# Making weight sums inside the up tiles: GpSimd's load queue, new row shapes, transposes, and a new order of products

## The chip, the cores and the metric

The kernel runs on one core of a Trainium2 chip. The core has five engines that work side by side: TensorE (PE in the profile; its weight loads are shown as PEld), VectorE (DVE), ScalarE (ACT), GpSimd (POOL) and SyncE (SP), and sixteen DMA engines that move data between the chip's memory (HBM) and the core's memory (SBUF). TensorE writes to PSUM, a small memory of eight banks. Each engine executes its own instructions in order; a DMA is issued by an engine's queue and lands later.

The metric is the time of one execution in microseconds of device time, and the median over runs.

## The reference, cut to what matters

A trunk of two layers on 256 tokens of width 2048, in float32. Each layer has a token mixer (first an mLSTM, then an HGRN2) and a gated MLP with a short convolution:

```python
def conv_glu(hn, w_up, conv_w, conv_b, w_down):
    u = hn @ w_up                       # (256, 2048) @ (2048, 11008)
    a, v = jnp.split(u, 2, axis=-1)
    ...
    c = conv_b
    for j in range(CONV_W):             # three taps
        c = c + ap[:, j:j + s] * conv_w[j]
    return (jax.nn.gelu(c, approximate=False) * v) @ w_down    # (256, 5504) @ (5504, 2048)

for layer in range(DEPTH):
    h = h + mix
    h = h + conv_glu(rmsnorm(h, norm_ffn_g[layer]), ffn_w_up[layer], ...)
```

The change touches only the gated MLP and its two matrix products.

## The kernel before, in words

**Precision by halves.** Every weight and activation is split into a rounded part and a remainder (`wh`, `wl`; `xh`, `xl`). A product is three matmuls, wh with xh, wl with xh, and wh with xl. For the weights the split is done on the chip (`halves`, L163): ScalarE copies a piece of 1024 columns to `wh` (L166), VectorE subtracts it from the raw weights to get `wl` (L167). There are four buffers of each (`WB`), and three raw buffers of 2048 columns (`RAW`), which SyncE's queue fills (L157 and L269). TensorE reads the pieces in order, so it can go on for as long as the pieces made ahead last.

**Stages of the MLP.** The 5504 hidden columns are 43 tiles of 128, in three parts of 16, 16 and 11 (`PARTS`). In each part an *up stage* comes first. One up tile is a chunk of kind "fm": 16 steps k over the width 2048, in each step two groups of columns (gate and value), and in each group one matmul of 512 columns (L436) and one of 256 (L439), 64 in all. Then `done_up` (L1100) scales, convolves, applies GELU, multiplies, and splits the result `g`. The second k step of the first up tile of each part is in a "turned" order, both products of 512 columns first and then both of 256 (`TURNS`, L424 to L433); other tiles of the mixers use this order too.

After the up stage come two *pairs* (`Pair`, `stream_pair`, L293), each of which makes 1024 of the 2048 output columns of the part's down product. A pair goes through its hidden tiles in couples. The letters of the plan tell how a couple is computed:

- N: two by two blocks of products, eight in all (H: the half of it).
- S: seven products instead of eight (a Strassen form). They need sums of the four blocks of weights, which `pair_sums` (L229) makes on VectorE in a buffer T4 just before they are used. The products go to four accumulators in two big PSUM tiles (c11, c12, c21, c22) and three small banks of their own (m1, m6, m7). At the last S or P `middle` adds the small ones to the residual stream `hx`, and at the pair's end `done` adds the big tiles (L1180).
- P: the same as S, but the sums were made ahead. The generator `sums_ahead` (L242) takes half a couple at a time: it loads it to the tile `pr0` with SyncE's queue (L253), makes the four sums in `pr1` (L230 to L232), splits them into `pr2` and `pr3` (L256, L257), and stores these two in HBM, in the array `sums`, with GpSimd's queue (L259). A row of such a load or store is 256 columns, 1 KB. When the pair arrives at the couple, GpSimd's queue loads the finished sums back into the same four tiles (L279), and the two plain blocks come through the raw buffers.

Each full pair has the plan PSNSPSNN with two P, each short one PSNNNH with one, and layer 1's last part has only one pair. That makes 19 couples, 38 halves.

**What sets the order.** `side.push` hands a generator to a little clock that advances by the estimated time of each product (`side.tick`); `sums_ahead` begins `REST` = 8 us after the part's first up tile by this clock and takes a half each `EACH` = 12 us. That is the order in which instructions are written. A planner then arranges each engine's instructions by their dependencies and its own estimate of times, and can take an instruction ahead of its place in the program where nothing that it depends on holds it back. On an engine's queue, what is behind a waiting instruction waits too.

Of the kernel before, what the change touches and what calls it, by code (L numbers as in the profile page):

```python
# [15 lines left out]
P = 128  # L16
# [5 lines left out]
TURNS = 1  # L22
# [6 lines left out]
REST = 8.0  # L29
EACH = 12.0  # L30
# [36 lines left out]
def trunk_kernel(ctx, tc, xT, x_d, fg_d, pp_d, cst_d, sel_d, w_gate, w_first, w_aq, w_ak, w_av, w_ao, w_aout,  # L67
# [64 lines left out]
    class Chunk:  # L132
        def __init__(self, kind, src, nk, x, done, before=None, last=False, turns=0):
            self.last, self.turns, self.apart = last, turns, False
            self.kind, self.src, self.nk, self.x, self.done, self.before = kind, src, nk, x, done, before
            self.width = {"fm": 256, "tm": 512, "first": 512}[kind]
# [26 lines left out]
    def halves(r, m):  # L163
        wh = wpool.tile([P, 1024], F32R, tag="wh", bufs=WB, name="wh")
        wl = wpool.tile([P, 1024], F32R, tag="wl", bufs=WB, name="wl")
        act.copy(wh[:, :m], r)  # L166
        dve.tensor_tensor(wl[:, :m], r, wh[:, :m].bitcast(F32), ALU.subtract)  # L167
# [74 lines left out]
    def sums_ahead(srcs, box):  # L242

        yield REST
        due, h = side.now, 256
        for n, src in srcs:
            for o in (0, h):
                while side.now < due and not side.flush:
                    yield 0.1
                due += EACH  # L250
                b, t, th, tl = (spare(i, box) for i in range(4))
                b, t = (v.bitcast(F32).rearrange("p (a b) -> p a b", a=4) for v in (b, t))
                nc.sync.dma_start(b, src.rearrange("p (a b) -> p a b", a=4)[:, :, o:o + h])  # L253
                pair_sums(b, t)
                t = t.rearrange("p a b -> p (a b)")
                act.copy(th, t)  # L256
                dve.tensor_tensor(tl, t, th.bitcast(F32), ALU.subtract)  # L257
                for j, v in enumerate((th, tl)):
                    pool.dma_start(sums[n, j].rearrange("p (a b) -> p a b", a=4)[:, :, o:o + h],  # L259
                                   v.rearrange("p (a b) -> p a b", a=4))  # L260
            stored.append(n)

    def split_pair(ch):
        w, b0 = ch.w, 0
        for kind in ch.plan:
            n = (2 if kind == "H" else 4) * w
            raw = wpool.tile([P, 2048], F32, tag="raw", bufs=RAW, name="raw")
            skip = w if kind == "P" else 0
            nc.sync.dma_start(raw[:, skip:n], ch.src[:, b0 + skip:b0 + n])  # L269
            c, b0 = b0 // n, b0 + n  # L270
            if kind == "P":
                yield halves(raw[:, w:3 * w], 2 * w)
                yield halves(raw[:, 3 * w:4 * w], w)
                n = ch.made[c]
                side.until(lambda: n in stored)
# [5 lines left out]
                continue  # L281
            if kind != "S":
# [10 lines left out]
    def stream_pair(ch, take):  # L293
# [5 lines left out]
        def product(name, x, wt, sp=False):  # L299
            (xh, xl), (wh, wl) = x, wt  # L300
            for i, (a, b) in enumerate(((xh, wh), (xh, wl), (xl, wh))):
                pe.matmul(acc[name][:, 0:w], a, b, start=name not in begun, stop=sp and i == 2)  # L302
# [6 lines left out]
        def part(u, i):  # L309
# [3 lines left out]
        for c, kind in enumerate(ch.plan):  # L313
            end = c == len(ch.plan) - 1
            if kind in "SP":
                kind = "S"
# [7 lines left out]
                u = take()  # L324
                product("m1", tok(k, 0), part(u, 0), fin)
                side.tick(0.68)
                product("c12", form(3), part(u, 1))
                side.tick(0.68)
                u = take()
                product("c11", tok(k + 1, 0), part(u, 0))  # L330
                side.tick(0.68)
                u = take()
                product("c22", form(0), part(u, 0), fin)
                if fin:
                    begun.discard("c22")
                side.tick(0.68)
                product("m7", form(2), part(u, 1), fin)
                side.tick(0.68)
                u = take()
                product("m6", form(1), part(u, 0), fin)  # L340
                side.tick(0.68)
                product("c21", tok(k + 1, 1), part(u, 1))
                if fin:
                    with tc.high_priority():
                        ch.middle(acc)
# [979 lines left out]
```

## Time and profile before

| | us |
|---|---|
| median of 3 runs | 2431.31 |
| lowest, highest run | 2430.45, 2440.63 |
| profiled execution, its own time | 2437.75 |
| its span, first to last instruction | 2435.7 |

| engine | instructions of the largest groups |
|---|---|
| TensorE | products of the "fm" tiles, L436 and L439, 3678 each |
| VectorE | remainders of weights, L167, 829 |
| ScalarE | rounded weights, L166, 829 |
| GpSimd | stores of sums, L259, 76, and loads of sums, L279, 76 |

The mean granted TensorE clock is 0.994 of full speed. The queue of SyncE moved 457.26 MB, GpSimd's 85.01 MB.

How to read the lines: a group or timeline line gives engine, line of the kernel, operation, what is written and read, and in brackets how long the engine was idle before it and what ended that. A line of stretches gives a stretch of time, and for each engine the busy time and number of instructions in it; then the granted clock, the mean busy share of the DMA engines and the GB/s moved. A product's busy time includes waiting in TensorE's pipe, so the number of matmuls in a stretch says more than their busy time.

### The profile page before, as it was taken

What the parts mean: (1) busy time and instruction counts of PE and PEld (TensorE: products, weight loads), DVE (VectorE), ACT (ScalarE), POOL (GpSimd) and SP (SyncE); (2) the same over time, 40 slices, a digit from 0 to 9 for tenths busy, and PEclk for the clock granted to TensorE, in tenths of its full rate; (3) what the DMA queues carried; (4) which work ended last, traced back from release to release, by engine and by line L of the source; (5) the groups of instructions that cost most, each with busy time, mean ns of one, the idle gap of its engine ahead of it and who ended that gap; (6) DMA issues with size and microseconds to landing.
All of it is one profiled execution on the core that took longest, in us unless ns stands there. A gap on an engine that the chain in (4) does not pass through costs nothing.

```text
span 2435.7 us, 37196 instructions
## 1 busy us (share of the span) xinstructions
PE 2398.5 (98%) x14200; PEld 2044.1 (84%) x14200; DVE 1937.7 (80%) x3159; ACT 1335.2 (55%) x2057; POOL 256.6 (11%) x375
## 2 busy tenths in 40 slices
PE   9999999999999999999999999998999999999998
PEld 7888878888888888878888888887888878888887
DVE  7766667778878788778888888886777878879776
ACT  6655556555456555555555555555555545554554
POOL 0100011000010011001222222211000101000000
PEclk9999999999999999999999999999999999999999
DMA  7654489556898589655444554449855789668744
GB/s 292 199 182 173 173 258 329 190 191 217 285 302 284 182 291 297 228 195 192 169 171 171 174 173 162 171 180 284 293 188 179 262 283 299 242 212 286 262 169 172
DMA packets 137633, 545.82 MB, mean 224 GB/s; under 512 B 10720, under 2 KB 69728, under 8 KB 86896
## 3 DMA queue, kind: packets, MB, share of 16 engines
q1 hardware_dynamic: 84288, 457.26, 53.2%
q0 software_dynamic: 52304, 85.01, 12.5%
q8 instruction: 111, 1.82, 0.3%
q10 hardware_dynamic: 864, 1.19, 0.1%
q14 instruction: 66, 0.54, 0.1%
HBM read 501.41 MB, written 42.01 MB: 223 GB/s over the span
## 4 chain that ended last, share of the span: by engine, by line
PE 80%; DMA 7%; DVE 6%; issue 4%; ACT 1%; POOL 0%; SPq 0%; POOLq 0%; ACTq 0%; DVEq 0%
PE mm L436 32%; PE mm L439 16%; PE mm L420 6%; PE mm L419 6%; PE mm L421 6%; PE c L302 6%; DVE wl L167 3%; DMA sums<-pr 3%; PE m L302 2%; DMA raw<-in_w_down 2%; DMA raw<-in_w_up 1%; ACT wh L166 1%; PE mm L428 1%; PE pn L785 1%; PE pd L968 1%
## 5 line engine op out<-in xcount | busy, mean ns | idle before, releaser
L436 PE MATMUL mm<-xt,wh 128*128 128x512 f32 x3678 | 1291.4, 396 | 1.8 <-ACT wh L166 1.8
L167 DVE TENSOR_TENSOR wl<-raw,wh 128x1024 fp32r<-128x1024 f32 (+1 forms) x829 | 990.9, 1200 | 321.3 <-ACT wh L166 314.0
L166 ACT CAST wh<-raw 128x1024 fp32r<-128x1024 f32 (+1 forms) x829 | 842.4, 1025 | 724.8 <-PE mm L436 422.2
L439 PE MATMUL mm<-xt,wl 128*128 128x256 f32 x3678 | 1026.4, 280 | 8.7 <-DVE wl L167 8.7
L436 PEld LDWEIGHTS mm<-xt,wh 128*128 128x128 f32 x3678 | 690.6, 188 | 162.2 <-ACT wh L166 3.4
L439 PEld LDWEIGHTS mm<-xt,wl 128*128 128x128 f32 x3678 | 694.2, 189 | 12.5 <-DVE wl L167 10.1
L302 PE MATMUL c<-wh,g 128*128 128x512 f32 x666 | 218.0, 390 | 0.0
L419 PE MATMUL mm<-wh,xt 128*128 128x512 f32 x480 | 188.1, 392 | 0.0
L420 PE MATMUL mm<-wl,xt 128*128 128x512 f32 x480 | 187.7, 391 | 0.0
L421 PE MATMUL mm<-wh,xt 128*128 128x512 f32 x480 | 187.3, 390 | 0.0
L302 PEld LDWEIGHTS c<-wh,g 128*128 128x128 f32 x666 | 125.3, 188 | 26.1
L302 PE MATMUL c<-wl,g 128*128 128x512 f32 x333 | 130.0, 390 | 0.0
L279 POOL DMA_DIRECT2D pr<-sums x76 | 40.9, 547 | 828.1 <-PE c L302 761.6
L421 PEld LDWEIGHTS mm<-wh,xt 128*128 128x128 f32 x480 | 90.2, 188 | 18.5
L419 PEld LDWEIGHTS mm<-wh,xt 128*128 128x128 f32 x480 | 90.1, 188 | 18.4
L420 PEld LDWEIGHTS mm<-wl,xt 128*128 128x128 f32 x480 | 90.1, 188 | 17.3
L257 DVE TENSOR_TENSOR pr<-pr,pr 128x1024 fp32r<-128x1024 f32 x38 | 46.4, 1222 | 72.1 <-DMA sums<-pr 59.8
L259 POOL DMA_DIRECT2D sums<-pr x76 | 54.2, 713 | 464.3 <-ACT pr L256 390.4
L166 ACT CAST wh<-T 128x1024 fp32r<-128x1024 f32 x54 | 56.1, 1051 | 71.4 <-PE c L302 37.9
L471 ACT COPY b<-mm 128x256 f32<-128x256 f32 x236 | 86.4, 366 | 14.3 <-DVE z L472 6.7
L167 DVE TENSOR_TENSOR wl<-T,wh 128x1024 fp32r<-128x1024 f32 x54 | 65.4, 1223 | 24.7 <-ACT wh L166 24.4
L256 ACT CAST pr<-pr 128x1024 fp32r<-128x1024 f32 x38 | 39.9, 1051 | 77.7 <-DMA sums<-pr 54.3
(269 smaller groups left out, 3001.2 us busy)
## 6 DMA issues: line engine op xcount, KB each, us to landing
raw<-in_w_up SPq DMA_DIRECT2D x172, 1024.0 KB, 5.0
raw<-in_w_down SPq DMA_DIRECT2D x60, 1024.0 KB, 4.9
raw<-in_w_bq SPq DMA_DIRECT2D x48, 1024.0 KB, 4.9
sums<-pr POOLq DMA_DIRECT2D x76, 512.0 KB, 8.3
pr<-sums POOLq DMA_DIRECT2D x76, 512.0 KB, 7.9
pr<-in_w_down SPq DMA_DIRECT2D x38, 512.0 KB, 5.3
raw<-in_w_ao SPq DMA_DIRECT2D x16, 1024.0 KB, 4.7
raw<-in_w_aout SPq DMA_DIRECT2D x16, 1024.0 KB, 6.4
```

The lines of the kernel that those rows point to most:

```text
L166: act.copy(wh[:, :m], r)
L167: dve.tensor_tensor(wl[:, :m], r, wh[:, :m].bitcast(F32), ALU.subtract)
L257: dve.tensor_tensor(tl, t, th.bitcast(F32), ALU.subtract)
L259: pool.dma_start(sums[n, j].rearrange("p (a b) -> p a b", a=4)[:, :, o:o + h], v.rearrange("p (a b) -> p a b", a=4))
L279: pool.dma_start(z[j], sums[n, j][:, 1024 * i:1024 * i + 1024])
L302: pe.matmul(acc[name][:, 0:w], a, b, start=name not in begun, stop=sp and i == 2)
L419: pe.matmul(ps[t], xh, wh[:, c], start=st, stop=False)
L420: pe.matmul(ps[t], xh, wl[:, c], start=False, stop=False)
L421: pe.matmul(ps[t], xl, wh[:, c], start=False, stop=sp)
L436: pe.matmul(ps[f], wh[:, c:c + P], x, start=st, stop=False)
L439: pe.matmul(ps[f][:, 0:T], wl[:, c:c + P], x[:, 0:T], start=False, stop=sp)
L471: act.copy(b, ps[:, T:2 * T])
```

## The change

Five things are different. The whole core of the diff follows.

1. `sums_ahead` is no generator on the clock any more. `done_up` calls it in chosen up tiles (`MAKE`: tiles 1, 2, 4, 5, 7, 8, 10, 11 of a part of 16; 1 to 4 of the part of 11), each time for one half couple. GpSimd first copies one column of that tile's output `c` into the load's buffer, and then issues the load, which therefore can't go before the tile's output is there. The load is on GpSimd's queue, no longer on SyncE's.
2. The weights of P couples are stored in HBM in another order (`_couples`), so that a half couple's row is 4 KB in one piece. The stores of the sums have rows of 2 KB. A P couple's two plain blocks and the first product's block now lie as two halves of 256 columns, so products of P couples read their 512 columns as two runs of 256.
3. In the first couple of each pair the products that go to the small banks come first: m1, m7, m6, c12, c11, c22, c21, where it was m1, c12, c11, c22, m7, m6, c21.
4. The turned order at the start of a part's first up tile is gone. In each up stage two transposes of a constant 128 x 128 matrix into a PSUM bank are put in that nobody reads (`RESETS`: before step k = 1 of tiles 2 and 9 in the first part, before k = 3 of tile 0 and k = 1 of tile 6 in the others).
5. The pool of the four `pr` tiles is opened with the MLP's other tiles.

```diff
-TURNS = 1
+RESETS = (((2, 1), (9, 1)), ((0, 3), (6, 1)), ((0, 3), (6, 1)))
...
-REST = 8.0
-EACH = 12.0
+MAKE = {16: (1, 2, 4, 5, 7, 8, 10, 11), 11: (1, 2, 3, 4)}
...
-    def sums_ahead(srcs, box):
-        yield REST
-        due, h = side.now, 256
-        for n, src in srcs:
-            for o in (0, h):
-                while side.now < due and not side.flush:
-                    yield 0.1
-                due += EACH
-                b, t, th, tl = (spare(i, box) for i in range(4))
-                b, t = (v.bitcast(F32).rearrange("p (a b) -> p a b", a=4) for v in (b, t))
-                nc.sync.dma_start(b, src.rearrange("p (a b) -> p a b", a=4)[:, :, o:o + h])
-                pair_sums(b, t)
...
-                for j, v in enumerate((th, tl)):
-                    pool.dma_start(sums[n, j].rearrange("p (a b) -> p a b", a=4)[:, :, o:o + h],
-                                   v.rearrange("p (a b) -> p a b", a=4))
-            stored.append(n)
+    def sums_ahead(n, src, o, box, after):
+        b, t, th, tl = (spare(i, box) for i in range(4))
+        b, t = (v.bitcast(F32).rearrange("p (a b) -> p a b", a=4) for v in (b, t))
+        pool.tensor_copy(b[:, 0, 0:1], after)
+        pool.dma_start(b, src.rearrange("p (o a b) -> p o a b", o=2, a=4)[:, o])
+        pair_sums(b, t)
+        t = t.rearrange("p a b -> p (a b)")
+        act.copy(th, t)
+        dve.tensor_tensor(tl, t, th.bitcast(F32), ALU.subtract)
+        for j, v in enumerate((th, tl)):
+            pool.dma_start(sums[n, j].rearrange("p (i o b) -> p i o b", i=2, o=2)[:, :, o],
+                           v.rearrange("p (i b) -> p i b", i=2))
+        stored.append((n, o))
...
             if kind == "P":
-                yield halves(raw[:, w:3 * w], 2 * w)
-                yield halves(raw[:, 3 * w:4 * w], w)
+                rows = raw[:, :1536].rearrange("p (o a b) -> p o a b", o=2, a=3)
+                nc.sync.dma_start(rows, src.rearrange("p (o a b) -> p o a b", o=2, a=4)[:, :, 1:4])
+                yield halves(rows[:, :, 0:2], 1024)
+                yield halves(rows[:, :, 2], 512)
...
-        def part(u, i):
+        def part(u, i, split=False):
+            if split:
+                return tuple(v.rearrange("p (o a b) -> p o a b", o=2, a=2)[:, :, i] for v in u)
...
+                steps = ("m1", "c12", "c11", "c22", "m7", "m6", "c21")
+                if c == 0:
+                    steps = ("m1", "m7", "m6", "c12", "c11", "c22", "c21")
...
+                        if k == ch.reset:
+                            pe.transpose(aux("turn")[:, 0:P], ident, ident)
...
+                if i in MAKE[GT.nf]:
+                    j = MAKE[GT.nf].index(i)
+                    if j // 2 < len(ahead):
+                        sums_ahead(*ahead[j // 2], j % 2, box, c[:, 0:1])
...
-                chunks.append(Chunk("fm", w_up[layer, f0 + i], KT, norm.x, done_up(f0 + i, i, GT), turns=1 if i < TURNS else 0))
+                chunks.append(Chunk("fm", w_up[layer, f0 + i], KT, norm.x, done_up(f0 + i, i, GT, ahead)))
+                chunks[-1].reset = dict(RESETS[part]).get(i)
...
+def _couples(w):
+    for f0, nf in PARTS:
+        for c, plan in enumerate((DOWN_PLAN[nf], DOWN_PLAN2[nf])):
+            for i, kind in enumerate(plan):
+                if kind == "P":
+                    v = w[:, c, :, (f0 + 2 * i) * 1024:(f0 + 2 * i + 2) * 1024]
+                    v[:] = v.reshape(2, P, 4, 2, 256).transpose(0, 1, 3, 2, 4).reshape(2, P, 2048)
+    return w
```

The planner still arranges the instructions of each engine; nothing else in the kernel is different.

81 lines of the change are left out of this document (35 added, 46 removed).

## The prediction

> **What bounds the kernel now.** I read the page first (parts 1 and 4), then the busy time by stretches, one stretch for each stage.
>
> ```profile
> span 2435.7 us, 37196 instructions
> PE 2398.5 (98%) x14200; PEld 2044.1 (84%) x14200; DVE 1937.7 (80%) x3159; ACT 1335.2 (55%) x2057; POOL 256.6 (11%) x375
> PE 80%; DMA 7%; DVE 6%; issue 4%; ACT 1%; POOL 0%; SPq 0%; POOLq 0%; ACTq 0%; DVEq 0%
> ```
>
> TensorE is the bound, and the number of its products hardly changes. So the change can only win time in which TensorE stands still, runs at a lower clock, or issues at a wider spacing. Part 4 puts some of that on DMA. The stretches say in which stages (275 to 401 is layer 0's mixer projection, 401 to 579 and 661 to 846 its first two up stages, 1583 to 1712 and 1976 to 2164 layer 1's projection and second up stage; 2368 to 2397 is the last pair):
>
> ```profile
> core 0: us, PE busy (x) PEld busy (x) DVE busy (x) ACT busy (x) POOL busy (x), PEclk, DMA share, GB/s
> 275.00:401.00 126.00, 121.80 (x565) 101.11 (x564) 88.43 (x136) 68.17 (x105) 13.80 (x20) 0.97 0.82 262
> 401.00:579.40 178.40, 178.40 (x1035) 156.19 (x1034) 136.76 (x226) 99.93 (x154) 2.29 (x4) 1.00 0.60 205
> 661.00:846.00 185.00, 180.69 (x1026) 156.87 (x1025) 150.21 (x245) 103.01 (x153) 12.09 (x18) 0.99 0.81 265
> 1583.00:1712.00 129.00, 122.73 (x762) 101.25 (x761) 97.22 (x168) 66.97 (x105) 20.05 (x25) 0.97 0.73 240
> 1976.00:2164.00 188.00, 182.72 (x1026) 157.82 (x1025) 150.14 (x245) 102.31 (x153) 12.10 (x18) 0.99 0.80 261
> 2368.00:2397.00 29.00, 29.00 (x130) 24.02 (x129) 23.39 (x29) 15.98 (x21) 0.53 (x1) 1.00 0.60 219
> ```
>
> Two up stages of 16 tiles each: the one without sums in it takes 178.4 us at a full clock, the one with them 185.0. Both projections have holes and a clock of 0.97, because the sums of each layer's first part are made there, ahead of their place in the program; the load of their weights has these first and last starts in 275 to 401:
>
> ```profile
> L253 SPq DMA_DIRECT2D pr<-in_w_down x8: 378/379/513, 316.1 to 382.5; - x8
> ```
>
> What such a hole is, the timeline of the second up stage shows (start, us, engine, line; in brackets the idle time and what ended it), and the chain of waits names what it hung on:
>
> ```profile
> 720.66 1.05 ACT L256 CAST pr<-pr 128x1024 fp32r<-128x1024 f32 x1 [6.57 <-DMA sums<-pr]
> 725.51 1.23 DVE L257 TENSOR_TENSOR pr<-pr,pr 128x1024 fp32r<-128x1024 f32 x1 [8.61 <-DMA sums<-pr]
> 727.93 0.39 PE L439 MATMUL mm<-xt,wl 128*128 128x256 f32 x1 [3.86 <-DVE wl L167]
> 708.39 17.03 DMA sums<-pr
> 345.20 14.30 DMA sums<-pr
> ```
>
> The store of one half's remainders took 17.03 us. The next half's subtraction writes the same buffer and waits for it at the head of VectorE's queue for 8.61 us; the weight remainders `wl` behind it are late, and TensorE stands for 3.86. So TensorE is covered for about 8.61 - 3.86 = 4.7 us. These are the six big holes, each in a stretch of 12 us:
>
> ```profile
> 356.00:368.00 12.00, 7.80 (x23) 5.69 (x22) 8.34 (x12) 8.83 (x15) 2.17 (x4) 0.72 0.83 242
> 1658.00:1670.00 12.00, 8.86 (x36) 6.84 (x35) 9.83 (x13) 7.04 (x12) 1.48 (x3) 0.86 0.75 218
> 1692.00:1704.00 12.00, 8.87 (x33) 6.81 (x32) 9.43 (x13) 7.14 (x11) 2.12 (x3) 0.86 0.81 247
> 722.00:734.00 12.00, 8.14 (x38) 6.80 (x37) 8.45 (x16) 6.07 (x11) 1.42 (x2) 0.86 0.65 190
> 2003.00:2015.00 12.00, 8.90 (x42) 7.49 (x41) 9.02 (x16) 5.94 (x11) 0.84 (x2) 0.86 0.65 190
> 2042.00:2054.00 12.00, 10.26 (x58) 8.49 (x57) 11.19 (x21) 7.80 (x12) 1.95 (x3) 1.00 0.84 255
> ```
>
> I price them by missing matmuls, which takes in the lower clock after a stop. A 512-column product takes 29.00/130 = 0.223 us undisturbed. In up stages, where 512 and 256 columns alternate, the mean is in the first of these rows, which also show a second, subtler loss:
>
> ```profile
> 420.00:568.00 148.00, 148.00 (x856) 129.44 (x856) 114.62 (x190) 83.41 (x128) 0.00 (x0) 1.00 0.56 193
> 675.00:715.00 40.00, 40.00 (x228) 34.68 (x227) 36.14 (x64) 23.87 (x34) 4.26 (x6) 1.00 1.04 326
> 1735.00:1883.00 148.00, 148.00 (x839) 128.34 (x838) 112.04 (x186) 80.83 (x127) 0.00 (x0) 1.00 0.55 190
> 2075.00:2160.00 85.00, 85.00 (x483) 73.65 (x482) 67.27 (x112) 47.23 (x74) 0.26 (x1) 1.00 0.61 209
> ```
>
> At full clock and with no hole, 148 us hold 856 matmuls in one up stage and 839 in another: 0.1729 against 0.1764 us. TensorE has two cadences here, and stays in one until something disturbs it.
>
> **The change, part by part.** *Loads to GpSimd's queue, one half couple per up tile.* The copy of one column of a tile's gated output into the load's buffer ties each half to its tile, so no sums are made in the projections any more, and SyncE's queue carries the stream of weights alone. What goes is the six holes: 12 - 23 x 0.223 = 6.9, 12 - 36 x 0.223 = 4.0, 12 - 33 x 0.223 = 4.6; with 0.173 for the up stages 5.4, 4.7 and 2.0. Together 27.6 us; the transposes among the 36 make this a little low.
>
> What comes in their place: the same 38 halves with the same VectorE and ScalarE work, now in up tiles of 64 x 0.173 = 11.1 us, in twos with a free tile between (four in a row in the 11-tile part). The old spacing was 12 us, and a store needs longer than its median in some cases:
>
> ```profile
> sums<-pr POOLq DMA_DIRECT2D x76, 512.0 KB, 8.3
> pr<-sums POOLq DMA_DIRECT2D x76, 512.0 KB, 7.9
> pr<-in_w_down SPq DMA_DIRECT2D x38, 512.0 KB, 5.3
> ```
>
> By the nearest row, the other 512 KB load on GpSimd's queue, the load lands after 7.9 us instead of 5.3; 2.6 more, inside the 4.7 of cover. DMA share is 0.56 without sums and 1.04 with them (675 to 715), so sums cost 0.48. Two tiles of three at 12/11.1 of the old rate give 0.56 + 0.48 x 2/3 x 12/11.1 = 0.91: below one, so that the backlog of two halves drains in the third tile; rows of 2 KB in the stores can only help. Bounds of the new holes: 0, and all 27.6. I take a quarter, 7 us: late stores of 14 to 17 us still reach past 11.1 + 4.7 now and then, and the 11-tile part has no free tile.
>
> On GpSimd the added wait on the tile's output holds up only what follows there: this half's load, its two stores, later the loads of finished sums. In the stage without sums GpSimd is busy 2.29 of 178.4 us, so its issue time costs nothing; without that cover it would be 38 x (0.694 + 0.538), 47 us:
>
> ```profile
> L639 POOL TENSOR_TENSOR rs<-rs,mhalf 128x2 f32<-128x2 f32 x24 | 16.6, 694 | 327.7 <-DVE rs L638 327.7
> L259 POOL DMA_DIRECT2D sums<-pr x76: 708/708/763, 322.7 to 2258.6; - x76
> L279 POOL DMA_DIRECT2D pr<-sums x76: 527/538/637, 393.3 to 2269.5; - x76
> ```
>
> Here the rule that speaks against this change: the Trainium skill, page "SBUF — State Buffer", section "SBUF: two separate sides", warns that a DMA on GpSimd's queue has its descriptors written by GpSimd, which some VectorE instructions lock out, and advises the SP or ACT queue. The trace does not show it: 76 issues lie between 708 and 763 ns while VectorE works 80% of the time. By the rule each load could be late by one VectorE instruction (1.23 us for L257), which is an estimate of 38 x 1.23 = 47 us on loads and, inside the cover, 0 on the sum.
>
> *Transposes instead of the turned order.* Twelve transposes (two in each of six up stages) replace the turned order at the second k step of every first up tile. Rows for other transposes (min/median/max ns), and in comparison a 256-column product (mean 280):
>
> ```profile
> L531 PE MATMUL pz<-cst,hx x96: 270/272/421, 330.8 to 1717.6; 128*128 128x128 f32 x96
> L439 PE MATMUL mm<-xt,wl 128*128 128x256 f32 x3678 | 1026.4, 280 | 8.7 <-DVE wl L167 8.7
> ```
>
> A transpose costs between nothing and a 256-column product, 2 x 0.1729 - 0.223 = 0.123 us; I take the upper end (272 is near 280), 1.5 us. If it sets the narrow cadence, the three slow rows give back (148 - 839 x 0.1729) + (85 - 483 x 0.1729) + (40 - 228 x 0.1729) = 2.9 + 1.5 + 0.6 = 5.0. Net 3.5 gained.
>
> *Small banks first.* In a pair's first couple m1, m7 and m6, which have small banks of their own, come before the four products into the big banks, which the previous pair's last addition still reads:
>
> ```profile
> PE c L302 <- DVE hx L1180: 3.0, 5, 1.0
> PEld c L302 <- DVE hx L1180: 5.1, 5, 1.4
> ```
>
> The first product into the big banks moves back by two products, 6 x 0.223 = 1.3 us, about the longest wait (1.0 and 1.4). Between 3.0 and 5.1 gained; I take 4.0. What is late next would be the stored sums, wanted 1.3 us earlier; they have been asked for a couple or more before.
>
> *Halves as 2 x 256.* Products of a sum made ahead now read their 512 columns in two runs, 342 of them (six products of three matmuls in 19 couples). No row shows such an operand. Bounds: 0, and two 256-column products for one of 512, 342 x (2 x 0.123 - 0.223) = 8 us. I take 0, as the columns are as many. The first banks of these couples come in two rows instead of one: same bytes, 0.
>
> Sum: -27.6 + 7 - 3.5 - 4.0 = -28.1. The profiled execution took 2437.75 us (span 2435.7 and 2.05 around it), which makes 2409.7. The runs' median is 2431.31, 6.4 below it; a run with smaller holes also has less to win, and from the median the sum would be 2403.2. I predict 2406, between the two.
>
> **The rivals.**
> (1) *The holes move along.* Store and load still share the engines with 2 MB of weights per tile; if the four up stages pay per half what they pay now, 27.6/38 = 0.73 us, only 7.5 us remain: 2424 to 2430. For it: the share of 1.04. Against: the free tiles.
> (2) *The transposes don't do it* and leave the wide cadence: 86 tiles x 64 x 0.0035 = 19 us instead of 5.0, so 2406 + 19 = 2425. For it: the cadence changed at disturbances of every kind. Against: fast tiles follow the transposes of the norm in the first up stage.
> (3) *Slower: GpSimd's queue in order.* The second half of two has its column copy and load behind the first half's stores, which wait for VectorE; the load lands late, its subtractions stand at VectorE's head beyond the 4.7 us, and TensorE stops once per second half, of which there are 20 (four in each 16-tile stage, three and one in the short ones). At the mean of the six holes, 4.6 us, eleven such stops (51 us) against the 35.1 us won make it slower, about 2447; all 20 give 2406 - 7 + 92 = 2491. For it: VectorE and ScalarE run in order, and a hole needs only 5 us. Against: stores of the first half are issued some 2 us after each other and before the next tile's end.
>
> **How the numbers follow.** My forecast 0.64, own range 2392 to 2418; rival 1 0.14; rival 2 0.08; rival 3 0.14. A measurement of this kernel can tell 0.5% from no change, 12 us: faster is under 2419, slower over 2443. Faster: the forecast and a little of 1 and 2, 0.67. Same: the rest of 1 and 2 and the mild end of 3, 0.19. Slower: 0.14. Range: below, no new hole, 5.1 for the banks and free transposes, 2431.3 - 27.6 - 5.0 - 5.1 = 2394, with 4 for small waits not listed 2390; above, rival 1 from the profiled execution with 8 us for split operands, 2437.75 - 7.5 + 8 = 2438.
>
> **What would show it.** Right: no sums in the projections, whose clock is 1.00 and whose length falls by 7 and 9 us; the three 16-tile stages with holes or wide cadence near 178 to 180 us; 856 matmuls in 148 us of every up stage; fewer than 2 us of TensorE waiting on L1180's successor. Wrong: VectorE or ScalarE waiting over 5 us for the load or the stores in most second halves, a DMA share over 1 across three tiles, or 839 in 148 us behind a transpose.

## The result, and the profile after

| | before | after |
|---|---|---|
| median of 5 runs, us | 2431.31 | 2455.34 |
| lowest, highest run | 2429.91, 2440.63 | 2451.77, 2461.19 |
| span of the profiled execution | 2435.7 | 2453.6 |

The ratio is 1.0089, with an interval of 1.0062 to 1.0116: slower, by 24 us, where 25 us less was forecast. The first lines and two groups of the page of after:

```profile
span 2453.6 us, 37312 instructions
PE 2402.9 (98%) x14212; PEld 2044.9 (83%) x14212; DVE 1926.6 (79%) x3159; ACT 1336.3 (54%) x2057; POOL 323.9 (13%) x451
...
L234 DVE TENSOR_TENSOR pr<-pr 128x512 f32<-128x512 f32 x38 | 26.3, 692 | 124.2 <-DMA pr<-in_w_down 124.0
...
L250 POOL COPY pr<-c 128x1 f32<-128x1 f32 x38 | 51.2, 1347 | 390.0 <-PE mm L436 313.5
```

TensorE is as busy as before. New is L234, the first subtraction of a half couple's sums: VectorE stood 124.0 us in front of it, for the load. The busy time by stretches of after, each stretch a stage:

```profile
275.60:394.00 118.40, 118.40 (x562) 99.08 (x561) 70.27 (x104) 60.59 (x96) 1.34 (x2) 1.00 0.52 177
394.00:581.90 187.90, 182.75 (x1039) 158.61 (x1038) 145.82 (x248) 106.82 (x161) 28.30 (x37) 0.99 0.76 251
...
665.60:851.60 186.00, 180.79 (x1027) 157.23 (x1026) 143.37 (x238) 102.47 (x152) 27.54 (x36) 0.99 0.77 255
...
937.50:1069.00 131.50, 126.09 (x707) 109.50 (x706) 98.13 (x155) 68.24 (x100) 15.89 (x20) 0.97 0.74 248
...
1598.70:1717.50 118.80, 118.80 (x761) 99.07 (x761) 83.30 (x140) 61.30 (x98) 10.78 (x12) 1.00 0.53 181
...
2177.90:2263.90 86.00, 83.46 (x356) 67.26 (x355) 77.74 (x90) 44.31 (x55) 6.36 (x12) 0.98 0.78 264
```

Both projections run without a hole, at a clock of 1.00. The up stages and pairs have holes now: the first stage with sums in it has 182.75 us of TensorE in 187.90. From the first product of a stage to that of the next, before and after, in us:

| stage | layer 0 | layer 1 |
|---|---|---|
| projection | 125.5, 118.4 | 129.0, 118.9 |
| up, first part | 178.9, 187.9 | 182.1, 186.2 |
| its pairs | 81.5, 83.7 | 81.9, 85.4 |
| up, second part | 185.0, 186.0 | 187.9, 188.8 |
| its pairs | 81.6, 85.8 | 81.1, 86.1 |
| up, third part | 122.4, 131.6 | 123.3, 122.3 |
| its pairs | 63.2, 59.4 | 28.6, 28.6 |

Projections -17.2, up stages +23.1, pairs +11.2: with 0.6 elsewhere, the 17.9 us by which the span is longer. The waits of after that bear on it (engine, what waited, line, what for; us in total, times, longest):

```profile
DVE pr L234 <- DMA pr<-in_w_down: 124.0, 36, 6.2
...
PEld mm L439 <- DVE wl L171: 23.1, 11, 3.5
PE mm L439 <- DVE wl L171: 19.7, 11, 3.2
...
PEld m L304 <- DMA pr<-sums: 8.0, 9, 1.1
...
PE mm L436 <- DVE v L472: 7.3, 4, 5.4
```

36 of 38 half couples make VectorE wait, and TensorE waits behind it for `wl` (L171 is the L167 of before) or for `v`, the emptying of a tile's banks. The eleven stops for `wl` all come behind second halves of couples, the four for `v` behind first halves. Together they are 27.0 us, all the time that TensorE stands in the up stages; after a stop the products also run at a lower clock for a while (0.97 to 0.99 in the three stretches of up stages above). The waits for stores are gone (59.8 us on VectorE and 54.3 on ScalarE before). The worst case stands in the 11-tile part; rows of the timeline of after:

```profile
995.81 1.22 DVE L171 TENSOR_TENSOR wl<-raw,wh 128x1024 fp32r<-128x1024 f32 x1
...
995.96 4.12 POOL L250 COPY pr<-c 128x1 f32<-128x1 f32 x1 [12.12 <-DVE pr L236]
...
999.96 0.41 DVE L472 TENSOR_TENSOR a<-mm,b 128x256 f32<-128x256 f32 x1
...
1000.38 0.54 POOL L251 DMA_DIRECT2D pr<-in_w_down  x1 [0.30 <-POOL pr L250]
...
1007.18 0.69 DVE L234 TENSOR_TENSOR pr<-pr 128x512 f32<-128x512 f32 x1 [6.21 <-DMA pr<-in_w_down]
...
1009.82 0.77 PE L436 MATMUL mm<-xt,wh 128*128 128x512 f32 x1 [5.41 <-DVE v L472]
1010.38 0.42 PE L439 MATMUL mm<-xt,wl 128*128 128x256 f32 x1
1010.60 0.63 PE L436 MATMUL mm<-xt,wh 128*128 128x512 f32 x1
```

The copy of one column takes 4.12 us on GpSimd. The copy had itself to wait for the half couple before, whose sums (L236) read the same buffer; four halves follow one another here without a free tile. The load goes out behind it at 1000.38 and lands after 6.7 us. Meanwhile VectorE stands for 6.21 us with the emptying of the last tile's banks (L472) behind the subtraction, and TensorE for 5.41; it comes back at a lower clock (0.70 in the mean from 1004.5 to 1015; the product at 1010.60 takes 0.63 us, where 0.40 is usual).

### The profile page after: what moved, and what is told of

It reads as the page before. It is cut to its first block, busy times and chain, and to the rows that moved or that the text cites. A ratio compares the mean times of both kernels' runs of the same rounds, so it can differ in the third digit from the quotient of the medians.

```text
span 2453.6 us, 37312 instructions
## 1 busy us (share of the span) xinstructions
PE 2402.9 (98%) x14212; PEld 2044.9 (83%) x14212; DVE 1926.6 (79%) x3159; ACT 1336.3 (54%) x2057; POOL 323.9 (13%) x451
## 3 DMA queue, kind: packets, MB, share of 16 engines
q1 hardware_dynamic: 66656, 437.34, 51.7%
## 5 line engine op out<-in xcount | busy, mean ns | idle before, releaser
L171 DVE TENSOR_TENSOR wl<-raw,wh 128x1024 fp32r<-128x1024 f32 (+1 forms) x829 | 988.1, 1197 | 292.1 <-ACT wh L170 288.5
L439 PE MATMUL mm<-xt,wl 128*128 128x256 f32 x3690 | 1034.1, 281 | 19.7 <-DVE wl L171 19.7
L439 PEld LDWEIGHTS mm<-xt,wl 128*128 128x128 f32 x3690 | 698.9, 190 | 24.6 <-DVE wl L171 23.1
L234 DVE TENSOR_TENSOR pr<-pr 128x512 f32<-128x512 f32 x38 | 26.3, 692 | 124.2 <-DMA pr<-in_w_down 124.0
L250 POOL COPY pr<-c 128x1 f32<-128x1 f32 x38 | 51.2, 1347 | 390.0 <-PE mm L436 313.5
L1119 ACT CAST g<-c 128x256 fp32r<-128x256 f32 x86 | 34.9, 405 | 101.4 <-DVE c L1117 100.8
L277 POOL DMA_DIRECT2D pr<-sums x76 | 41.3, 551 | 327.2 <-PE c L304 226.6
```

Source lines behind the costliest of these rows:

```text
L171: dve.tensor_tensor(l, r, h.bitcast(F32), ALU.subtract)
L250: pool.tensor_copy(b[:, 0, 0:1], after)
L277: pool.dma_start(z[j], sums[n, j][:, 1024 * i:1024 * i + 1024])
L439: pe.matmul(ps[f][:, 0:T], wl[:, c:c + P], x[:, 0:T], start=False, stop=sp)
```

## The experiments

The theory: the late load at the head of VectorE's queue costs the time; the rest of the change is worth what was forecast or nothing. Against it: the new order, the rows, or sums in up tiles as such. All times are medians beside runs of before on the same chip (2431.31 for after, 2427.42 for e1 to e4, 2432.08 for e5, e6, e8 and the kernel without transposes, 2429.87 for the last four rows). The third column is the interval of the ratio to these. Stage columns are differences, in us, of one profiled execution from that of before; e2 and e8 show by how much before's own holes move from one execution to the next, and e1's profiled execution (2467.2) was above its median.

| kernel | us | ratio, 95% | wait for the load, us | projections | up | pairs |
|---|---|---|---|---|---|---|
| after | 2455.34 | 1.0062-1.0116 | 124.0 | -17.2 | +23.1 | +11.2 |
| e1_old_order | 2452.74 | 1.0079-1.0139 | 134.4 | -17.2 | +32.0 | +12.6 |
| e2_only_order | 2432.0 | 0.9991-1.0035 | 8.9 | -5.7 | -2.4 | -2.5 |
| e3_load_on_sync | 2401.17 | 0.9863-0.9912 | 65.1 | -17.2 | -16.9 | +0.4 |
| e4_load_a_tile_ahead | 2400.21 | 0.9859-0.9912 | none | -17.2 | -18.2 | -3.1 |
| e5_first_half_on_sync | 2441.33 | 1.0022-1.0066 | 120.6 | -17.2 | +18.1 | +9.7 |
| e6_copy_by_vector | 2428.7 | 0.9957-0.9999 | 88.6 | -17.2 | -6.8 | +10.5 |
| e8_rows_only | 2429.9 | 0.9968-1.0012 | 7.7 | -0.7 | -8.8 | -2.4 |
| e10_ahead_no_transposes | 2397.0 | 0.9818-0.9883 | none | -17.2 | -22.6 | +1.3 |
| e9_sums_twice | 2413.46 | 0.9905-0.9953 | 25.1 | -17.2 | -17.9 | +9.2 |
| e10_sums_four_times | 2556.79 | 1.0496-1.0544 | 23.5 | -17.2 | +28.1 | +108.3 |
| e11_only_place_and_lead | 2396.24 | 0.9838-0.9883 | none | -17.2 | -22.6 | -3.4 |
| e12_no_tie | 2418.23 | 0.9937-0.9974 | 17.4 | -15.6 | -6.1 | +0.9 |

**The order of products.** e1 takes it out of after, e2 puts it alone into before.

```diff
-                if c == 0:
-                    steps = ("m1", "m7", "m6", "c12", "c11", "c22", "c21")
```

> The changed kernel with the products of a pair's first couple in the old order again (m1, c12, c11, c22, m7, m6, c21); all else as changed. In the changed kernel the seven full pairs' stages together grew by 11.2 us (first pairs' starts wait for the stored sums, 3.8 and 8.0 us of PE waits; the big banks' waits grew from 3.0 and 5.1 to 5.1 and 7.0). Theory A (the new order asks for the sums, and so the raw pieces behind them, too early): pairs fall back by 8 to 11 us, total about 2445. Rival B (the pairs are late because the sums are finished late in the up stage, whatever the order): pairs stay within 3 us of the changed kernel, total about 2453.

```diff
-                product("m1", tok(k, 0), part(u, 0), fin)
...
+                steps = ("m1", "c12", "c11", "c22", "m7", "m6", "c21")
+                if c == 0:
+                    steps = ("m1", "m7", "m6", "c12", "c11", "c22", "c21")
```

> The kernel before with only the products of a pair's first couple in the new order. Theory A: the order itself costs, the pairs grow by 8 us or more, total about 2440. Rival B: the order alone is neutral or gains up to 4 us (waits on L1180's successor under 3 us), total 2427 to 2432.

e1 is as slow as after, e2 as fast as before. The short pairs of layer 0 take 59.5 us in e2, 3.7 less than in before; but with the old order they take 60.0 in e8, 60.7 in e1 and 60.9 in e11, so the order is worth about 1 us there at most, and before's 63.2 holds a stop of its own (1.4 us for late weights, and a clock of 0.97). The timeline of before shows why the order does so little, at the start of the second pair:

```profile
619.32 0.39 PE L302 MATMUL c<-wh,g 128*128 128x512 f32 x1
619.55 0.39 PE L302 MATMUL m<-wh,g 128*128 128x512 f32 x1
...
620.23 1.52 PE L302 MATMUL m<-pr,F 128*128 128x512 f32 x6
...
622.62 0.50 PE L302 MATMUL c<-wh,F 128*128 128x512 f32 x1 [0.65 <-DVE hx L1180]
```

Products into small banks (`m`), six of them from sums made ahead, already stand ahead of the first into a big one (`c`): the planner had made much the same order by itself, and the wait for the last addition is still there behind them. In e4, with the new order, TensorE still waits 3.6 us for that addition (3.0 in before).

**The load on SyncE's queue, or a tile ahead.** e3 changes only the queue; e4 issues the load one up tile earlier, still on GpSimd's queue, and ties the sums to their tile by a column copy on VectorE.

```diff
-        pool.dma_start(b, src.rearrange("p (o a b) -> p o a b", o=2, a=4)[:, o])
+        nc.sync.dma_start(b, src.rearrange("p (o a b) -> p o a b", o=2, a=4)[:, o])
```

> The changed kernel with the half couples' load on SyncE's queue; it still waits for GpSimd's copy of the tile's output column. VectorE waits 124 us in 36 places for this load in the changed kernel. Theory A (GpSimd's queue is what makes it late: 7.8 us to landing against 5.3): the wait falls to about 124 - 38 x 2.5 = 30 us, total about 2440. Rival B (the tie to the same tile's output makes it late, on any queue): the wait stays over 80 us, and the stream of weights behind the tied load on SyncE's queue is late too; total 2450 or more.

```diff
-    def sums_ahead(n, src, o, box, after):
+    def load_ahead(n, src, o, box, after):
...
+        loaded.append((n, o, b))
+    def sums_ahead(box, after):
+        n, o, b = loaded.pop()
...
+        dve.tensor_copy(t[:, 0, 0:1], after)
...
-                if i in MAKE[GT.nf]:
-                    j = MAKE[GT.nf].index(i)
+                if loaded and i in MAKE[GT.nf]:
+                    sums_ahead(box, c[:, 0:1])
+                if i + 1 in MAKE[GT.nf]:
+                    j = MAKE[GT.nf].index(i + 1)
```

> The changed kernel with each half couple's load one up tile earlier than its sums: the load is tied to the tile before (GpSimd's copy, GpSimd's queue, as changed), the sums to the tile they were tied to (a one-column copy by VectorE itself). Theory A (the loss in up stages is VectorE standing at the head of its queue for a load issued only one landing before): VectorE's wait for the load falls from 124 to under 15 us, TensorE's waits on L171 and on v from 27 to under 8 us, up stages fall by 15 to 20 us in sum, total about 2437. Rival B (the loss is the sums' own work and traffic in the up tiles): up stages stay within 5 us, total over 2449.

Both are 26 to 27 us faster than before, and far under the time that the theory gave them: the place was right, the size too small. e4 has no wait for the load at all, and the up stages and the pairs lose what they had gained. Nor did the queue as such do it: in e4 it is GpSimd's, and the load lands after 4.0 us (median; 3.8 for first halves, 6.6 for second). But e3 is as fast as e4 with 65.1 us of waiting. Why half the waits cost nothing, the three-tile stretches of the first up stage show, after first, then e4:

```profile
418.00:451.00 33.00, 33.00 (x193) 28.88 (x192) 26.29 (x46) 19.18 (x29) 3.84 (x6) 1.00 0.73 234
451.00:484.00 33.00, 33.00 (x193) 28.88 (x192) 28.82 (x50) 20.38 (x31) 7.37 (x8) 1.00 0.82 264
484.00:517.00 33.00, 32.02 (x184) 27.53 (x183) 26.87 (x47) 18.70 (x28) 6.32 (x8) 1.00 0.77 253
517.00:550.00 33.00, 30.56 (x173) 26.24 (x173) 25.00 (x45) 16.90 (x26) 4.03 (x7) 1.00 0.73 240
```

```profile
484.00:517.00 33.00, 33.00 (x191) 28.71 (x190) 29.04 (x51) 19.81 (x30) 5.28 (x8) 1.00 0.87 276
517.00:550.00 33.00, 33.00 (x189) 28.62 (x188) 30.02 (x55) 20.76 (x31) 5.05 (x10) 1.00 0.89 281
```

and VectorE's waits, for after in the last three of its stretches, for e4 in its two:

```profile
DVE pr L234 <- DMA pr<-in_w_down: 3.3, 1, 3.3
...
DVE pr L234 <- DMA pr<-in_w_down: 6.7, 2, 4.5
...
DVE pr L234 <- DMA pr<-in_w_down: 7.9, 2, 5.1
```

```profile
DVE wl L171 <- ACT wh L170: 3.9, 6, 1.2
...
DVE wl L171 <- ACT wh L170: 2.7, 6, 0.7
```

In e4 VectorE works 29.0 to 30.0 of 33 us, and some 3 us are spare (it waits for ScalarE's next piece, which comes as buffers come free). After asks for 6.7 and 7.9 us of waiting in that place. A single wait of 3.3 us, as in 451 to 484, is paid from the spare time and costs no product. From the third couple on products fall from 193 to 184 and 173; that the pieces made ahead are used up by then is how I read it, as the buffers' filling itself is in no view. In e3 the waits in such stretches are 1 to 5 us.

The pairs lose too. GpSimd's rows at the end of layer 1's second up stage, in after (pair from 2177.9 us) and e4 (pair from 2128.45):

```profile
2164.62 0.70 POOL L257 DMA_DIRECT2D sums<-pr  x1 [1.17 <-DVE pr L255]
...
2176.32 0.53 POOL L277 DMA_DIRECT2D pr<-sums  x1 [2.78 <-DMA sums<-pr]
```

```profile
2101.76 0.69 POOL L266 DMA_DIRECT2D sums<-pr  x1 [0.77 <-DVE pr L264]
...
2109.52 0.53 POOL L286 DMA_DIRECT2D pr<-sums  x1 [0.68 <-DMA sums<-pr]
```

The part's last store is issued 13.3 us before the pair in after and 26.7 in e4, so the last of the finished sums for the first couple are asked for 1.6 us before the pair instead of 18.9. TensorE waits for such loads 3.8 us in all (8.0 on its weight loads, in the row above). In the pairs it stands 11.6 us in after and 3.6 in e4; what else makes up the 14.3 us between them was not taken apart.

**What makes the load late.** e5 puts first halves on SyncE's queue, e6 lets VectorE copy the column, e12 leaves the copy out.

```diff
-        pool.dma_start(b, src.rearrange("p (o a b) -> p o a b", o=2, a=4)[:, o])
+        (pool if o else nc.sync).dma_start(b, src.rearrange("p (o a b) -> p o a b", o=2, a=4)[:, o])
```

> The changed kernel with the load of the first half of each couple on SyncE's queue, of the second half on GpSimd's: half the dose. VectorE waits 124 us for all loads in the changed kernel, 65 us with all on SyncE's queue (total 2401). In three up tiles (33 us) VectorE has 2.4 to 3.9 us to spare. Theory A (a budget: waits cost nothing until they use up that spare time, then all of the rest): waits of about 95 us, or 5 us in three tiles, about 1.5 us over the spare time in some 14 groups of three tiles; total 2412 to 2422. Rival B (each wait costs its own part): half way, about 2428. Rival C (a wait costs when it is itself over 4.7 us): second halves wait 3 to 5.6 us as before, few over 4.7; total below 2410.

```diff
-        pool.tensor_copy(b[:, 0, 0:1], after)
+        dve.tensor_copy(b[:, 0, 0:1], after)
```

> The changed kernel with the one-column copy that ties the load done by VectorE instead of GpSimd; the load stays on GpSimd's queue. GpSimd's copy takes 1.35 us in the mean (214 to 4124 ns) in the changed kernel and stands ahead of the load. Theory A (that copy is part of what makes the load late): the wait for the load falls by about 38 x 1.2 = 45 us to about 80 us, total 2405 to 2420. Rival B (only the landing on that queue, behind the stores, is late): the wait stays over 105 us, total over 2440.

```diff
-        pool.tensor_copy(b[:, 0, 0:1], after)
```

> The changed kernel without the column copy that ties the load to a tile's output; GpSimd's queue, rows, order and transposes as changed. The planner can then take loads and sums ahead of their tile. Theory A (a load tied to the tile of its sums is what makes VectorE wait): VectorE's wait for the load falls under 50 us in the up stages; the sums of each first part go back into the projections, which grow by 5 to 10 us each; total 2410 to 2430. Rival B (GpSimd's queue alone is the loss): the wait stays near 124 us, total over 2445.

Landing after issue, and waiting at L234, by halves, worked out from each load and its subtraction in the traces:

| | first halves: landing (median), waiting | second halves |
|---|---|---|
| after | 5.8, 45.1 us | 8.5, 79.1 us |
| e5 (first on SyncE) | 5.4, 40.1 | 9.1, 80.4 |
| e3 (both on SyncE) | 5.8, 36.8 | 6.3, 28.4 |
| e6 (copy on VectorE) | 5.5, 28.5 | 9.5, 60.5 |

First halves land alike on either queue, so e5 takes away almost none of the waiting, and its expected fall did not come. All three forecasts for its time missed: 2441.33 is above the budget's 2412 to 2422, above half way (2428), and above 2410. Yet it is 9.3 us over before where after is 24.0: of the 7.3 us between their profiled spans, 5.7 are in layer 0's 11-tile part, whose worst stop is 1.85 us in e5, not 5.41. So the sum of the waits alone does not give the time. Second halves, issued 1.5 to 3.4 us behind two stores of 512 KB, take over 2 us longer on GpSimd's queue than on SyncE's. e6 takes the other delay away: the copy, of which the rows for after and then e6 say (min/median/max ns):

```profile
L250 POOL COPY pr<-c x38: 214/1197/4124, 426.2 to 2309.0; 128x1 f32<-128x1 f32 x38
L251 POOL DMA_DIRECT2D pr<-in_w_down x38: 535/552/637, 426.7 to 2311.6; - x38
```

```profile
L250 DVE COPY pr<-c x38: 145/150/159, 426.3 to 2279.1; 128x1 f32<-128x1 f32 x38
```

With 35 us less waiting e6 is 27 us faster than after; it lies above the 2405 to 2420 expected with the copy as a part of the cause; its pairs still lose 10.5. So the load is late by three things: the copy (e6), its place behind the stores on GpSimd's queue (e3 against after), and that it is asked for only when its tile is done (e4). Its subtraction stands in VectorE's order as if it had landed; that the planner's estimate of landing is too short is a reading, not a measurement. In e12 loads may go early: the waiting falls to 17.4 us, but waits for the stores return (31.3 on ScalarE, 27.7 on VectorE). The sums of each first part went back into the projections, as expected (layer 0's eight loads are issued from 318.4 to 385.3 us, before the up stage, and seven of layer 1's eight before 1698), but the projections are only 0.5 and 1.1 us longer than in after, where 5 to 10 each were expected. So the tie is what keeps the halves at their tiles, and sums made in a projection need not cost what they cost in before.

**Rows, transposes, and sums in up tiles as such.** e8 puts the rows and two-run operands alone into before. The next is e4 without transposes and with the turned order, two things at once; from it the last two compute the same sums two and four times.

```diff
-                nc.sync.dma_start(b, src.rearrange("p (a b) -> p a b", a=4)[:, :, o:o + h])
+                nc.sync.dma_start(b, src.rearrange("p (o a b) -> p o a b", o=2, a=4)[:, o])
...
-                product("m1", tok(k, 0), part(u, 0), fin)
+                product("m1", tok(k, 0), part(u, 0, split), fin)
...
+        w_down=_couples(np.stack([_pairs(A(ffn_w_down)[i]) for i in range(2)])),
```

> The kernel before with only the new layout: loads of half couples in rows of 4 KB, stores of sums in rows of 2 KB, P couples' products in two runs of 256; queues, times and order as before. Theory A (the wider rows make the stores land sooner, and the six holes of before were late stores): longest landing from 17 to under 12 us, VectorE's and ScalarE's waits for stores from 59.8 and 54.3 to under 30 each, total 2405 to 2415. Rival B (the stores were late because of the spacing and the crowd on the DMA engines, not the rows): holes stay, total over 2422. In both the two-run operands cost nothing: pairs unchanged.

```diff
-                        if k == ch.reset:
-                            pe.transpose(aux("turn")[:, 0:P], ident, ident)
...
+                chunks.append(Chunk("fm", w_up[layer, f0 + i], KT, norm.x, done_up(f0 + i, i, GT, ahead), turns=1 if i < 1 else 0))
```

> The kernel with the load a tile ahead (2400.2 us), without its twelve transposes and with the turned order in each part's first up tile as before. A transpose adds 121 ns in the trace of the changed kernel (k steps of 727 and 780 instead of 693 twice). Theory A (the transposes set the narrow cadence, 0.214 us a tile): without them some stages run wide, at least 15 tiles of 86; total 2402 to 2410. Rival B (with no holes the cadence stays narrow anyway): total 2399, by the 1.5 us of the transposes.

```diff
-        pair_sums(b, t)
+        for _ in range(2):
+            pair_sums(b, t)
```

> The kernel with the load a tile ahead and without transposes (2397.0 us), in which the sums of each half (the three subtractions of pair_sums on VectorE, about 1.27 us) are made twice, with the same result: 2.5 us more of VectorE's time in three up tiles, no wait added. VectorE has 2.4 to 3.9 us to spare there. Theory A (budget of spare time): no more than 4 us longer, under 2402. Rival B (what costs is a wait for a landing, work costs nothing at any amount) says the same here and differs in the next run. Rival C (any work on VectorE in up tiles costs its own time): 38 x 1.27 = 48 us, 2445.

```diff
-        pair_sums(b, t)
+        for _ in range(4):
+            pair_sums(b, t)
```

> The same with the sums made four times: 3.8 us more per half, 7.6 us in three up tiles. Theory A (budget): 7.6 less about 3 to spare, 4.6 us in each of some 13 groups of three tiles, 60 us: 2440 to 2470. Rival B (only waits for a landing cost): under 2410.

e8 changes nothing in the time that can be measured: its longest store still takes 14.1 us, against 17.0, and the waits for stores are 40.1 us on VectorE and 43.4 on ScalarE, against 59.8 and 54.3 in before and 58.6 and 51.7 in e2. Without transposes and with the turned order the up stages of e4 become 4.4 us shorter; the medians differ by 3.2, less than the intervals can tell apart. Stretches of 148 us of the two first up stages, in e4 and then without transposes:

```profile
415.30:563.30 148.00, 148.00 (x849) 128.90 (x848) 130.63 (x228) 90.94 (x136) 21.37 (x36) 1.00 0.89 289
...
1707.80:1855.80 148.00, 148.00 (x849) 128.90 (x848) 130.54 (x228) 90.93 (x136) 21.41 (x36) 1.00 0.88 288
```

```profile
413.10:561.10 148.00, 148.00 (x856) 129.43 (x855) 131.76 (x230) 91.44 (x136) 21.38 (x36) 1.00 0.89 291
...
1704.00:1852.00 148.00, 148.00 (x857) 129.50 (x856) 131.75 (x230) 91.97 (x137) 21.40 (x36) 1.00 0.88 291
```

856 products in 148 us come with the turned order and no holes; with the transposes it is 849. The 849 is a mean of two spacings. In e4 the transposes of the first up stage run at 420.08 and 497.85 us; these are stretches of 66 us before and behind the second:

```profile
430.00:496.00 66.00, 66.00 (x383) 57.65 (x382) 59.22 (x105) 40.54 (x61) 9.63 (x16) 1.00 0.88 284
510.00:576.00 66.00, 66.00 (x376) 57.20 (x375) 56.68 (x97) 37.64 (x57) 7.86 (x14) 1.00 0.89 289
```

From tile 3 on a tile takes 11.09 us up to the second transpose and 11.31 behind it, in both layers, and in e3 as well; without the transposes it is 11.09 to the end. In an estimate from these, tiles 9 to 15 at 0.22 us more in two layers, and twelve transposes at 0.121 each, make 3.1 + 1.5 = 4.6 us, near the 4.4. So a transpose can set the wide spacing, with no hole near it. In the second and third parts the planner took both transposes to the start of the stage, that of tile 6 too (658.39 and 658.50 us in e4, whose stage begins at 657.93), and the spacing stays narrow behind them.

Sums made twice raise VectorE's busy time from 1938.9 to 1975.6 us, 37 more, and cost 16 us, where under 2402 was expected; made four times (2076.3, 137 more) they cost 160, above the 2440 to 2470 expected. In the up stages alone the budget of spare time comes near: 4.7 us more with sums made twice (at most 4 expected) and 50.7 with four (60 expected), though the latter come mostly as one long stop in tile 12 of each 16-tile stage and not in each group of three tiles. The larger part of both misses lies in the pairs, 7.9 and 107.0 us more, which wait for sums stored late; the wait in the kernel with four:

```profile
PE m L314 <- DMA pr<-sums: 68.1, 14, 15.0
```

So the up stages have room for the sums once, not for much more, and what comes too late there is paid in the pairs.

**The best of it.** e11 is before with two things alone: sums made in the up tiles of `MAKE`, and the load issued a tile ahead on GpSimd's queue. Rows of 1 KB, the old order and the turns stay.

```diff
-        yield REST
...
-                nc.sync.dma_start(b, src.rearrange("p (a b) -> p a b", a=4)[:, :, o:o + h])
+    def load_ahead(n, src, o, box, after):
+        b = spare(0, box).bitcast(F32).rearrange("p (a b) -> p a b", a=4)
+        pool.tensor_copy(b[:, 0, 0:1], after)
+        pool.dma_start(b, src.rearrange("p (a b) -> p a b", a=4)[:, :, 256 * o:256 * o + 256])
+        loaded.append((n, o, b))
```

> The kernel before with only two things changed: sums are made in the same up tiles as in the changed kernel, and their load goes one up tile ahead (tied to the tile before by GpSimd's column copy, on GpSimd's queue). Rows of 1 KB, order of products and the turned order stay as before, no transposes. Theory A (place and lead are all that is worth anything; wider rows, the written order and the transposes are not): 2394 to 2401. Rival B (the 2 KB rows are needed for one half per up tile, whose stores would be late else): VectorE and ScalarE wait over 30 us for stores again, 2405 or more.

2396.24 us, as the theory expected: 33.6 under before beside it, and faster than both kernels. Its span is 42.9 us under that of before's profile (-17.2, -22.6, -3.4 by stages, with 0.3 elsewhere). VectorE and ScalarE wait neither for loads nor for stores of sums, though the longest store still takes 15.2 us.

## Why the prediction was wrong, step by step

*The step that failed* is the cost of the load: "2.6 more, inside the 4.7 of cover", from which "7 us" of new holes followed. Between e4, whose load is on time, and after lie 54.0 us of span: 41.3 in the up stages, 14.3 in the pairs, less 1.7 at the start, where e4 begins later. The landing itself came as forecast (7.8 us median, against 7.9). Three other things were wrong in the step. The delay: copy (mean 1.35 us, not 0.69), issue and landing all come after the tile's output, while SyncE's load of before could run ahead of its use (VectorE waited 6.3 us for it in all). The cover: 4.7 us was taken from one wait. By the same difference, VectorE's wait less TensorE's stop, it was 2.3 to 4.0 us at the eleven stops for `wl` (5.56 - 3.22 and 4.45 - 0.47 at the ends); 36 waits in a row draw on the same buffers, which VectorE refills from some 3 us of spare time in 33. So only three of the nineteen second halves waited over the 5 us that the prediction named as its sign, and eleven stopped TensorE. And the step asked only how long the landing takes, not how early the planner puts the subtraction.

*GpSimd's issue and copy at nothing* was wrong in the same way: GpSimd has time, but the copy stands in the chain from tile to load. *Sums asked for a couple ahead* did not hold in after, where the last load of the first couple went out 1.6 us before the pair, and 18.9 us before it in e4; the pairs' +11.2 was in no case of the prediction.

*The third rival* had the mechanism right: GpSimd's queue, the load behind the first half's stores, the subtraction at VectorE's head, TensorE stopped behind second halves. It gave 2447 for eleven stops of 4.6 us; TensorE's stops for `wl` were eleven, all behind second halves, but of 3.2 us at most and 19.7 in all, and 2455 was measured, so the like number of stops is a coincidence. First halves wait too (45.1 us), which it left out, and four of them stop TensorE for 7.3 us. The argument against it, that stores are issued before the next tile's end, held by some 0.04 us (the second store's issue begins that much before the tile's output). The copy then starts 0.5 us behind the output; what took long was the copy itself and the landing.

*The six holes, -27.6*, was right in its size and place, for the execution that was profiled. The projections lost 7.1 and 10.1 us (7 and 9 forecast), and with the load on time the second up stages lose 7.4 and 10.4 (e11), the cadence among it. *Waits for stores* went as well.

*Transposes, -3.5*, had the wrong sign in a kernel without holes: +4.4 in the up stages of e4 against the same with the turned order in their place. They were to set the narrow cadence, and the one in tile 9 set the wide one. With the turned order and no holes (e11) layer 1's first up stage, at 839 products in before, has 856. Behind holes and behind a transpose the cadence was seen to change; which way it goes each time stays open. *The second rival*, that the transposes leave the wide cadence, was right for the tiles from 9 on. *The first rival*, that the holes move along, is not seen once the load is on time: e4's up stages have no stop, at a DMA share of 0.88 to 0.89 in 148 us (0.91 forecast).

*Small banks first, -4.0*, is 0 in full pairs and about -1 in layer 0's short pairs. The step took the order on TensorE from the program's text; the timeline of before had the other.

*Two-run operands and rows at 0* held (e8, ratio 0.9968 to 1.0012).

Without the late load e4 is 27.2 us under before beside it, and e11 33.6. That e4 meets the sum of -28.1 is in part luck: the +7, -3.5 and -4.0 beside the holes were each wrong, and they come to -0.5 together.

## What to carry to other kernels

A load that is tied to the end of a tile is best issued a tile before its use, or at least on a queue with no stores ahead of it; its price is the whole chain (tie, queue, landing) against the place where its user stands in an in-order queue. Cover for one wait is not cover for thirty: compare the waits of a stretch with the spare time of the waiting engine in that stretch. And read the executed order from the timeline before pricing a new order of the program's text.

## What the runs showed of the hardware

- A copy of one column (128 x 1) on GpSimd took 0.2 to 4.1 us. In the timeline above it ended as VectorE turned from instructions with two inputs in SBUF to L472, which reads `mm` in PSUM. All 38 copies of after end 0.04 to 0.05 us behind the end of a VectorE instruction with two inputs in SBUF; the one of 4.12 us lasts through six of them in a row, and the eight copies of e4 that met no VectorE instruction took 0.18 us. The Trainium skill, page "SBUF — State Buffer", section "Who interferes with whom", states that a VectorE instruction with two SBUF inputs contends with a GpSimd instruction that reads SBUF, and calls the ports that they share an exclusive lock. These ends agree with it, though no run was made for that alone. Issues of loads were not lengthened (535 to 637 ns), so the 1.23 us a load of the prediction's estimate is not seen in them.
- 512 KB on GpSimd's queue landed in 5.8 us (median) for first halves and in 8.5 behind two stores (after), and in 3.8 and 6.6 when asked for a tile ahead (e4). In e4 no store was issued in the 10 us ahead of a second half's load; of eleven with the next store 0.5 us behind them, ten took 6.6 to 7.0 us, and the eight with it 1.4 to 1.5 us behind took 3.7 to 4.7. So stores close by on the queue go with a late landing, ahead or behind; how a queue shares the DMA engines was not tried by itself.
- TensorE alternating 512 and 256 columns has two spacings, 856 and 839 products in 148 us (11.09 and 11.31 us for a tile of 64), both at a clock of 1.00 and both held over whole stages. A hole or a transpose can change the one into the other. What decides was not found.
